# RWKV-7 scan on Trainium2: the triangles of the inversion go through DRAM to one head per partition

## The chip, the cores and the metric

The kernel runs on one core of a Trainium2 chip. The metric is the device time in microseconds of one execution. A run of the kernel is compared with runs of the other kernel on the same chip.

## What is computed

One inference step of a two-layer hybrid trunk over 640 tokens (a prompt of 128 and a sample of 512), width 1024: layer 0 has grouped-query attention beside a Mamba-2 scan, layer 1 a bidirectional RWKV-7 time mixing, and both have a SwiGLU feed-forward part. The change lies in the scan of layer 1, which in the reference is this, for 16 heads of 64, once forward and once backward over the tokens:

```python
def rwkv7_scan(r, w, k, v, kk, a, s0):
    def step(S, inp):
        r_t, w_t, k_t, v_t, kk_t, a_t = inp
        sa = jnp.einsum('bhvk,bhk->bhv', S, kk_t)
        S = (S * w_t[:, :, None, :] - sa[..., None] * (kk_t * a_t)[:, :, None, :]
             + v_t[..., None] * k_t[:, :, None, :])
        return S, jnp.einsum('bhvk,bhk->bhv', S, r_t)
```

## The kernel before

The engines are TensorE (PE; PEld is its weight load), VectorE (DVE), ScalarE (ACT), GpSimd (POOL) and SyncE (SP), which issues most DMAs. Each runs its own stream of instructions in order. The kernel is written in a framework that assigns buffers and sets the order of each engine's stream from the order of the program and from its own costs of instructions; so an edit at one place can move instructions at others.

**The scan in chunks.** The 640 tokens of a direction are cut into five blocks of 128, each of two chunks of 64 (`par` 0 and 1). A chunk is done for all 16 heads at once in matrix form: the recurrence within it becomes a triangular system of 64 equations per head. Work goes by pairs of blocks: block 0 of both directions first (the prompt), then the forward block i with the backward block 5 - i, five pairs in all, numbered 0 to 4.

**`prep` (L1491)** makes what a block needs. It loads the decays into `th` (L1499) and the keys into `kb` (L1508), multiplies `th` by a cumulative matrix (`pc`, L1504), takes exponentials on ACT (L1506 and L1507) into `P` and `Pi`, loads `ar` (L1518) and scales `ar` and `kb` with them (L1520, L1521, L1523; the table `ENGS` says for each whether DVE or POOL does it). Then, per chunk, 32 matmuls give `pS` (L1534), the products of all heads, and DVE multiplies them with a mask (L1536; "the masks", eight per chunk) into the tile `sc`. For three of four pairs of buffers `sc` is a tile of its own, for the others a part of `xt_`, so rows carry either name. Last, `kb` is transposed (`pT`, L1541) and copied to `bt` on ACT (L1542).

**`invert` (L1545)** inverts the 64 triangles of a pair (two directions, two chunks, 16 heads). The two 32x32 diagonal blocks of each go into the buffer `nu`, one head and chunk per partition: 128 partitions are two directions by two halves by 32 heads and chunks. Four DVE stream transposes of 32x1024 (L1555) bring them there from `sc`, where the row index of the triangle lies on the partitions. Then 31 column steps on DVE (a product L1562 and a subtraction L1564 each) build the inverses in `wu`, two more transposes (L1568 into `nu`'s place, L1569) turn them back, and the off-diagonal blocks come from two rounds of small matmuls, `pX` (L1577) and `pW` (L1585), with ACT copies between and after them (L1579, L1589, L1593) that write the inverses back into `sc`. `nu` is read by pX, pW and L1593 until the end of an inversion.

**`chain` (L1595)** is the sequential part: per chunk `pR`, `pU`, `pY`, `pN` on PE with ACT copies between them, and the update of the state `S` on DVE (L1666, L1667). The chain of pair i needs the inverses of pair i and the state of pair i - 1.

**The order.** The driving loop (L1800) interleaves the chain of pair i, the inversion of pair i + 1 and the prep of pairs i + 1 and i + 2 by a string of letters per pair, `SEQS` (L1684); each letter advances one generator by a piece. Pair 0 is prepared and inverted ahead of the loop, while PE computes the values v (`pz`, L1709). In what follows turn i is the stretch in which pair i is inverted, from the end of the column steps of pair i - 1 to the end of its own.

The pool `psc` has two PSUM banks, shared by `pc`, `pT`, `pX` and `pW`.

Of the kernel before, what the change touches and what calls it, by code (L numbers as in the profile page):

```python
# [9 lines left out]
F32 = mybir.dt.float32  # L10
# [78 lines left out]
def _build(ctx, tc, I, O):  # L89
# [38 lines left out]
    thd = dram.tile([2, 5, 128, 1024], F32, name="thd")  # L128
    vd = dram.tile([5, 128, 1024], F32, name="vd")
    yd = dram.tile([2, 10, 64, 1024], F32, name="yd")  # L130
    gd = dram.tile([KT, 128, NT], F32, name="gd")
    xd = dram.tile([128, KT, NT], F32, name="xd")

# [1333 lines left out]
    if True:  # L1467
# [23 lines left out]
        def prep(d, blk, us, bi=0):  # L1491
# [3 lines left out]
            else:  # L1495
                sc = scp[npair[0] // 2 % 2].tile([128, 2, 16, 128], F32, name="sc", tag="sc")
            ap = arp[npair[0] // 2 % 2]
            npair[0] += 1
            load(th, thd[d, blk])  # L1499
            P, Pi, kb = Ps[d], Pis[d], kbs[d]  # L1500
            for q in range(2):
# [8 lines left out]
            for par in range(2):  # L1510
                c = blk * 2 + par
                pl = ap.tile([128, 8, 1], F32, name="pl", tag="pl")
                e = 64 if d == 0 else 1
                G.tensor_copy(pl, P[:, :, par, e:e + 1])
                ar = ap.tile([128, 8, 128], F32, name="ar", tag="ar")
                bk = kb[:, :, par, :]
                o = 0 if d == 0 else 2
                load(ar, rkd[:, :, c].rearrange("p m s t -> p m (s t)"))  # L1518
                ea, eb, ec = ((V, G)[int(z)] for z in ENGS[bi][3 * d:3 * d + 3])
                ea.tensor_tensor(out=ar[:, :, 0:64], in0=P[:, :, par, o:o + 64], in1=ar[:, :, 0:64], op=ALU.mult)  # L1520
                eb.tensor_tensor(out=ar[:, :, 64:128], in0=P[:, :, par, 1:65], in1=ar[:, :, 64:128], op=ALU.mult)  # L1521
                bkv = bk.rearrange("p m (s t) -> p m s t", s=2)
                ec.tensor_tensor(out=bkv, in0=bkv, in1=Pi[:, :, par, :].unsqueeze(2).to_broadcast([128, 8, 2, 64]), op=ALU.mult)  # L1523
                us.append((sc, ar, ap.tile([128, 1024], F32, name="bt", tag="bt"), pl, c, par))
                yield
            for sc, ar, bt, _, _, par in us:
                bk = kb[:, :, par, :]
                for g4 in range(2):

                    pS = [pry.tile([128, 4, 128], F32, name="pS", tag="r") for _ in range(2)]  # L1530
                    for m in range(4):
                        for i in range(2):
                            r = slice(i * 64, i * 64 + 64)
                            T.matmul(pS[i][:, m], bk[r, g4 * 4 + m, :], ar[r, g4 * 4 + m], start=True, stop=True)  # L1534
                    for i in range(2):
                        V.tensor_tensor(out=sc[:, par, g4 * 8 + i:g4 * 8 + 8:2, :], in0=pS[i],  # L1536
                                        in1=msk[d].unsqueeze(1).to_broadcast([128, 4, 128]), op=ALU.mult)
                for g2 in range(2):
                    pT = psc.tile([128, 512], F32, name="pT", tag="s")
                    for m in range(4):  # L1540
                        lastp[0] = T.transpose(pT[:, m * 128:(m + 1) * 128], bk[:, g2 * 4 + m, :], ident)  # L1541
                    S.copy(bt[:, g2 * 512:(g2 + 1) * 512], pT)  # L1542
                yield

        def invert(pairs):  # L1545


            place = ((0, 96), (64, 32))
            G.memset(wu, 0.0)
            G.memset(wu.rearrange("p a b -> p (a b)")[:, 0:1024:33], 1.0)  # L1550
            for g, sc in enumerate(pairs):
                for hf in range(2):
                    r0 = place[g][hf]
                    o = nu[r0:r0 + 32]
                    V.transpose(o if g == 0 else o.rearrange("p j t -> p t j"),  # L1555
                                sc[hf * 32:hf * 32 + 32, :, :, hf * 32:hf * 32 + 32].rearrange("p a h t -> p t (a h)"))
            for j in range(31):
                if j % 8 == 0:
                    yield
# [35 lines left out]
        def chain(us, fresh, ry, keep=False):  # L1595
# [59 lines left out]
            firsts = start_states(pY, hi)  # L1655
            yield
            for d, u in enumerate(us):
                _, _, bt, pl, _, _ = u
                pN = psu.tile([128, 8, 64], F32, name="pN", tag="u")
                for hd in range(16):  # L1660
                    r0 = 64 * (hd % 2)
                    T.matmul(pN[r0:r0 + 64, hd // 2, :], bt[:, hd * 64:(hd + 1) * 64], uvs[d][:, hd, :], start=True, stop=True)
                if fresh:
                    V.tensor_tensor(out=sst[d], in0=pN, in1=pl.to_broadcast([128, 8, 64]), op=ALU.mult)
                else:
                    V.tensor_tensor(out=sst[d], in0=pN, in1=sst[d], op=ALU.add)  # L1666
                    V.tensor_tensor(out=sst[d], in0=sst[d], in1=pl.to_broadcast([128, 8, 64]), op=ALU.mult)  # L1667
                yield
# [25 lines left out]
        uf, ub = [], []  # L1694
        for _ in itertools.chain(prep(0, 0, uf), prep(1, 0, ub)):
            pass
        inv_ = invert((uf[0][0], ub[0][0]))
        for _ in inv_:
            pass

# [99 lines left out]
        for bt_ in range(5):  # L1800
# [30 lines left out]
            for t in SEQS[bt_]:  # L1831
                if t == 's':
                    next(inv_, None)
                elif t == 'i':
                    inv_ = invert((nf[0][0], nb[0][0]))
                    next(inv_)
                elif t == 'j':
                    next(inv_)
# [112 lines left out]
```

## Time and profile before

| | |
|---|---|
| median of three runs | 2121.82 us (2121.23 to 2124.61) |
| profiled execution | 2116.96 us, span of its trace 2115.2 us |
| busy in the span | PE 1950.7 us (92%), DVE 1447.0 (68%), ACT 940.2 (44%), POOL 560.6 (27%) |
| DMA queue of SP and other hardware rings (q1) | 208.87 MB, 32.9% of 16 engines |
| ACT's DMA queue (q10) | 13.11 MB in 17280 packets, 2.0% |

The scan takes some 370 of the 2115 us, from about 1158 to 1530. Shares over the whole span say little of it, because the feed-forward parts and projections on both sides of it are long runs of matmuls. So the rows below are a table of busy time by stage, and the order in time of single engines. In a timeline row the first number is the start, the second the time of the row's instructions together; "[2.43 <-PE pW L1585]" says that the engine sat idle for 2.43 us before it and that PE's pW at line 1585 ended this.

### The profile page before, as it was taken

The page shows a single profiled execution, that of the slowest core. Times are in us where ns is not written, and L with a number is a line of the kernel's source. Part 1 is how long each engine was busy: PE and PEld are TensorE (multiplying, and loading weights), DVE is VectorE, ACT ScalarE, POOL GpSimd, SP SyncE. Part 2 cuts the span into 40 slices and gives each one's busy share as a digit, 9 for nine tenths or more (in the row PEclk, how much of TensorE's full clock was granted, in tenths as well). Part 3 has the DMA queues.
Part 4 walks back from the last instruction along what each step waited for, and adds up shares of the span by engine and source line. Part 5 has one row for each costly group of instructions (what it writes and reads, how often), then busy time and mean ns, then how long its engine had stood idle before and what let it go on. Part 6 is the DMA issues. An engine that isn't in the chain of part 4 may idle for free. (4 is left out here: it accounts for less than half of the span.)

```text
span 2115.2 us, 42931 instructions
## 1 busy us (share of the span) xinstructions
PE 1950.7 (92%) x17701; PEld 1785.1 (84%) x17701; DVE 1447.0 (68%) x2589; ACT 940.2 (44%) x1734; POOL 560.6 (27%) x510
## 2 busy tenths in 40 slices
PE   6999988999999999989999897877789999999998
PEld 5888766989999999969677786867779899999998
DVE  4474666467666758587676839889956787666675
ACT  4333454253433525355555343544463535344351
POOL 2111331002424326031234123313321025243330
PEclk8999999999999999989997988878889899999999
DMA  9764000422433524342466634425344322323221
GB/s 295 220 201 115 7 1 21 149 90 81 130 120 90 162 67 121 108 122 65 148 206 224 202 105 134 123 78 152 100 141 123 120 81 80 100 66 95 61 90 50
DMA packets 256408, 245.72 MB, mean 116 GB/s; under 512 B 27850, under 2 KB 217299, under 8 KB 256085
## 3 DMA queue, kind: packets, MB, share of 16 engines
q1 hardware_dynamic: 233076, 208.87, 32.9%
q0 software_dynamic: 5856, 21.01, 3.0%
q10 hardware_dynamic: 17280, 13.11, 2.0%
q8 instruction: 139, 2.28, 0.5%
q14 instruction: 57, 0.46, 0.1%
HBM read 203.76 MB, written 39.19 MB: 115 GB/s over the span
## 5 line engine op out<-in xcount | busy, mean ns | idle before, releaser
L979 DVE TENSOR_TENSOR ol<-wr,oh 128x512 fp32r<-128x512 f32 x344 | 316.1, 935 | 101.0 <-ACT oh L978 93.6
L978 ACT CAST oh<-wr 128x512 fp32r<-128x512 f32 x344 | 211.3, 619 | 307.1 <-PE d L1130 174.7
L1130 PE MATMUL d<-hid,oh 128*128 128x320 f32 x1312 | 291.3, 310 | 3.6 <-ACT hid L1027 2.5
L1130 PEld LDWEIGHTS d<-hid,oh 128*128 128x128 f32 x1312 | 220.5, 188 | 5.2 <-ACT hid L1027 3.2
L1130 PE MATMUL d<-hid,ol 128*128 128x320 f32 x656 | 203.0, 309 | 0.0
L443 DVE SCALAR_TENSOR_TENSOR x<-d,mod,x 128x128 f32<-128x128 f32 (+2 forms) x204 | 77.2, 433 | 141.6 <-PE d L1130 116.1
L1000 POOL TENSOR_TENSOR g<-wr 128x512 f32<-128x512 f32 x36 | 48.4, 1344 | 460.0 <-DMA wr<-in_ffn_w_up_dram 280.8
L1130 PEld LDWEIGHTS d<-hid,ol 128*128 128x128 f32 x656 | 123.6, 188 | 0.0
L401 PE MATMUL d<-hh,wh 128*128 128x320 f32 (+1 forms) x464 | 118.7, 328 | 3.5 <-ACT hh L435 1.6
L401 PE MATMUL d<-hl,wh 128*128 128x320 f32 (+1 forms) x464 | 114.2, 317 | 3.8 <-POOL hl L436 3.2
L401 PE MATMUL d<-hh,wl 128*128 128x320 f32 (+1 forms) x464 | 112.9, 315 | 0.0
L388 DVE TENSOR_TENSOR wl<-wr,wh 128x1024 fp32r<-128x1024 f32 (+1 forms) x57 | 70.1, 1230 | 56.9 <-ACT wh L386 56.4
L386 ACT CAST wh<-wr 128x1024 fp32r<-128x1024 f32 (+1 forms) x57 | 58.8, 1035 | 105.1 <-PE d L401 65.7
L401 PEld LDWEIGHTS d<-hh,wh 128*128 128x128 f32 (+1 forms) x464 | 79.7, 190 | 17.2 <-ACT at L1385 4.1
L401 PEld LDWEIGHTS d<-hl,wh 128*128 128x128 f32 (+1 forms) x464 | 79.2, 189 | 8.5 <-POOL hl L436 5.9
L1027 ACT CAST hid<-e 128x320 fp32r<-128x320 f32 x88 | 40.5, 460 | 101.4 <-DVE e L1045 100.9
L401 PEld LDWEIGHTS d<-hh,wl 128*128 128x128 f32 (+1 forms) x464 | 79.2, 189 | 1.6 <-DVE wl L388 0.6
L1534 PE MATMUL pS<-ar,ta 64*128 64x128 f32 x640 | 56.4, 311 | 21.4 <-POOL uv L1602 10.2
L1003 POOL TENSOR_TENSOR wr<-wr 128x512 f32<-128x512 f32 x36 | 50.6, 1409 | 84.9 <-DVE ol L979 57.0
L1534 PEld LDWEIGHTS pS<-ar,ta 64*128 64x128 f32 x640 | 48.5, 213 | 28.6 <-POOL uv L1602 11.1
L1005 POOL TENSOR_TENSOR wr<-wr 128x512 f32<-128x512 f32 x36 | 53.3, 1492 | 66.4 <-DVE ol L979 66.4
L1562 DVE TENSOR_TENSOR xt__11664<-ta 128x31 f32<-128x31 f32 (+15 forms) x155 | 66.4, 429 | 4.4 <-ACT ta L1760 0.2
(630 smaller groups left out, 5997.5 us busy)
## 6 DMA issues: line engine op xcount, KB each, us to landing
wt<-in_mod_w_dram SPq DMA_DIRECT2D x80, 512.0 KB, 4.3
wr<-in_ffn_w_gate_dram SPq DMA_DIRECT2D x44, 512.0 KB, 4.4
wr<-in_ffn_w_up_dram SPq DMA_DIRECT2D x44, 512.0 KB, 5.2
wr<-in_ffn_w_down_dram SPq DMA_DIRECT2D x44, 512.0 KB, 4.2
ta<-kbd SPq DMA_DIRECT2D x10, 1024.0 KB, 6.2
ar<-rkd SPq DMA_DIRECT2D x20, 512.0 KB, 5.6
wr<-in_ab_w_in_dram SPq DMA_DIRECT2D x16, 512.0 KB, 7.1
wt<-in_mod_w_dram SPq DMA_DIRECT2D x6, 1024.0 KB, 8.9
```

Of the source, the lines that this page charges most:

```text
L386: S.copy(wh, wr)
L388: V.tensor_sub(wl, wr, wh.bitcast(F32))
L401: T.matmul(ps[b][0:cn, 0:320], w[:, k, 0:cn], a[:, t0:t1], start=(k == 0 and i == 0), stop=(k == w.shape[1] - 1 and i == 2))
L443: V.scalar_tensor_tensor(out=x[:, k, c0:c1], in0=ps[b][:, c0 - 320 * b:c1 - 320 * b], scalar=mod[:, layer, v, gcol + k:gcol + k + 1], in1= ...
L978: S.copy(hi, src)
L979: V.tensor_tensor(out=lo, in0=src, in1=hi.bitcast(F32), op=ALU.subtract)
L1000: E.tensor_tensor(out=g3, in0=a11, in1=a21, op=ALU.add)
L1003: E.tensor_tensor(out=a11, in0=a11, in1=a21, op=ALU.add)
L1005: E.tensor_tensor(out=a12, in0=a12, in1=a11, op=ALU.add)
L1130: T.matmul(bank[:, 0:c1 - c0], p, q, start=i == 0 and z == 0, stop=i == n - 1 and z == 2)
L1534: T.matmul(pS[i][:, m], bk[r, g4 * 4 + m, :], ar[r, g4 * 4 + m], start=True, stop=True)
L1562: V.tensor_tensor(out=tv, in0=nu[:, j + 1:32, j:j + 1].to_broadcast([128, n, j + 1]), in1=wu[:, j:j + 1, 0:j + 1].to_broadcast([128, n, j ...
```

## The change

The tiles of the triangles reach `nu` by way of DRAM instead of by the four DVE transposes. Ten DRAM tiles `nd` are added, one per block and direction, with the layout row, chunk, head, column.

For the backward direction (d = 1), SP writes the masked triangle from `sc` to `nd`, one DMA per chunk in runs of 256 bytes (1024 of them). For the forward direction the triangle is needed transposed, so PE computes the product a second time with its operands exchanged: `pQ`, 16 matmuls of 64x64 per chunk. ACT copies it into `nt`, which is the memory of `th`, and two DMAs of ACT's queue write it to `nd`, in runs of 256 bytes (512 each). No mask is applied to it; the column steps read only the part strictly below the diagonal. `invert` then loads `nu` with four SP DMAs of 32x32x32, in runs of 128 bytes (1024 each). Since `nt` is the memory of `th`, the next load of `th` waits for the two writes out of it; since `nu` is read until the end of the inversion before, its loads wait for that.

In all: 20 DVE transposes fewer; 160 matmuls pQ, 10 ACT copies, 20 DMA issues on ACT and 30 on SP more. Lines behind the edit move by 13 (L1562 becomes L1575, L1666 becomes L1679), those of prep by 3 (L1536 becomes L1539).

```diff
--- before.py
+++ after.py
@@ -128,6 +128,7 @@
     thd = dram.tile([2, 5, 128, 1024], F32, name="thd")
     vd = dram.tile([5, 128, 1024], F32, name="vd")
     yd = dram.tile([2, 10, 64, 1024], F32, name="yd")
+    nd = [dram.tile([64, 2, 16, 64], F32, name=f"nd{i}") for i in range(10)]
     gd = dram.tile([KT, 128, NT], F32, name="gd")
     xd = dram.tile([128, KT, NT], F32, name="xd")
 
@@ -1495,7 +1496,9 @@
             else:
                 sc = scp[npair[0] // 2 % 2].tile([128, 2, 16, 128], F32, name="sc", tag="sc")
             ap = arp[npair[0] // 2 % 2]
+            n_ = nd[npair[0]]
             npair[0] += 1
+            nt = th.rearrange("p (a m s) -> p a m s", a=2, m=8)
             load(th, thd[d, blk])
             P, Pi, kb = Ps[d], Pis[d], kbs[d]
             for q in range(2):
@@ -1521,9 +1524,9 @@
                 eb.tensor_tensor(out=ar[:, :, 64:128], in0=P[:, :, par, 1:65], in1=ar[:, :, 64:128], op=ALU.mult)
                 bkv = bk.rearrange("p m (s t) -> p m s t", s=2)
                 ec.tensor_tensor(out=bkv, in0=bkv, in1=Pi[:, :, par, :].unsqueeze(2).to_broadcast([128, 8, 2, 64]), op=ALU.mult)
-                us.append((sc, ar, ap.tile([128, 1024], F32, name="bt", tag="bt"), pl, c, par))
+                us.append((sc, ar, ap.tile([128, 1024], F32, name="bt", tag="bt"), pl, c, par, n_))
                 yield
-            for sc, ar, bt, _, _, par in us:
+            for sc, ar, bt, _, _, par, _ in us:
                 bk = kb[:, :, par, :]
                 for g4 in range(2):
 
@@ -1535,6 +1538,18 @@
                     for i in range(2):
                         V.tensor_tensor(out=sc[:, par, g4 * 8 + i:g4 * 8 + 8:2, :], in0=pS[i],
                                         in1=msk[d].unsqueeze(1).to_broadcast([128, 4, 128]), op=ALU.mult)
+
+                if d == 0:
+                    pQ = psc.tile([128, 8, 64], F32, name="pQ", tag="s")
+                    for m in range(8):
+                        for i in range(2):
+                            r = slice(i * 64, i * 64 + 64)
+                            T.matmul(pQ[r, m, :], ar[r, m, 0:64], bk[r, m, 0:64], start=True, stop=True)
+                    S.copy(nt[:, par], pQ)
+                    for i in range(2):
+                        nc.scalar.dma_start(out=n_[:, par, i:16:2, :], in_=nt[i * 64:i * 64 + 64, par])
+                else:
+                    load(n_[:, par], sc[0:64, par, :, 0:64])
                 for g2 in range(2):
                     pT = psc.tile([128, 512], F32, name="pT", tag="s")
                     for m in range(4):
@@ -1542,18 +1557,16 @@
                     S.copy(bt[:, g2 * 512:(g2 + 1) * 512], pT)
                 yield
 
-        def invert(pairs):
+        def invert(pairs, nds):
 
 
             place = ((0, 96), (64, 32))
             G.memset(wu, 0.0)
             G.memset(wu.rearrange("p a b -> p (a b)")[:, 0:1024:33], 1.0)
-            for g, sc in enumerate(pairs):
+            for g in range(2):
                 for hf in range(2):
-                    r0 = place[g][hf]
-                    o = nu[r0:r0 + 32]
-                    V.transpose(o if g == 0 else o.rearrange("p j t -> p t j"),
-                                sc[hf * 32:hf * 32 + 32, :, :, hf * 32:hf * 32 + 32].rearrange("p a h t -> p t (a h)"))
+                    r0, b = place[g][hf], slice(hf * 32, hf * 32 + 32)
+                    load(nu[r0:r0 + 32], nds[g][b, :, :, b].rearrange("i a h j -> (a h) i j"))
             for j in range(31):
                 if j % 8 == 0:
                     yield
@@ -1655,7 +1668,7 @@
             firsts = start_states(pY, hi)
             yield
             for d, u in enumerate(us):
-                _, _, bt, pl, _, _ = u
+                _, _, bt, pl, _, _, _ = u
                 pN = psu.tile([128, 8, 64], F32, name="pN", tag="u")
                 for hd in range(16):
                     r0 = 64 * (hd % 2)
@@ -1694,7 +1707,7 @@
         uf, ub = [], []
         for _ in itertools.chain(prep(0, 0, uf), prep(1, 0, ub)):
             pass
-        inv_ = invert((uf[0][0], ub[0][0]))
+        inv_ = invert((uf[0][0], ub[0][0]), (uf[0][6], ub[0][6]))
         for _ in inv_:
             pass
 
@@ -1832,7 +1845,7 @@
                 if t == 's':
                     next(inv_, None)
                 elif t == 'i':
-                    inv_ = invert((nf[0][0], nb[0][0]))
+                    inv_ = invert((nf[0][0], nb[0][0]), (nf[0][6], nb[0][6]))
                     next(inv_)
                 elif t == 'j':
                     next(inv_)
```

The change also moves other instructions. Three places follow, all on DVE.

DVE in turn 1, before: the masks of pair 1 (L1536), the transposes (L1555), and the first column step (L1562, 128x31).

```order
L1536 TENSOR_TENSOR xt__11664<-pS,ta 128x4x128 x8
L1555 STREAM_TRANSPOSE ta<-xt__11664 32x32x32 x2
L1536 TENSOR_TENSOR sc<-pS,ta 128x4x128 x4
L1555 STREAM_TRANSPOSE ta<-sc 32x1024 x2
L1521 TENSOR_TENSOR ar<-ta,ar 128x8x64
L1562 TENSOR_TENSOR xt__11664<-ta 128x31
```

The same place in the changed kernel; L1539 are the masks, L1679 and L1680 the update of the two directions' states in the chain of pair 0, L1575 the column step.

```order
L1539 TENSOR_TENSOR xt__11674<-pS,ta 128x4x128 x8
L1539 TENSOR_TENSOR sc<-pS,ta 128x4x128 x4
L1679 TENSOR_TENSOR S_12769<-pN,S_12769 128x512
L1680 TENSOR_TENSOR S_12769<-S_12769,pl 128x512
L1524 TENSOR_TENSOR ar<-ta,ar 128x8x64 x2
L1679 TENSOR_TENSOR S_12770<-pN,S_12770 128x512
L1680 TENSOR_TENSOR S_12770<-S_12770,pl 128x512
L1539 TENSOR_TENSOR sc<-pS,ta 128x4x128 x3
L1575 TENSOR_TENSOR xt__11674<-ta 128x31
```

The updates, which stood among the later column steps (from the 15th on), now stand ahead of the first, and with them two products of `ar` and three masks of pair 2.

DVE at the start of turn 2, before: the transposes back, the four transposes of the new pair, and the first steps.

```order
L1568 STREAM_TRANSPOSE ta<-ta 128x1024
L1569 STREAM_TRANSPOSE xt__11664<-ta 128x1024
L1555 STREAM_TRANSPOSE ta<-sc 32x32x32
L1555 STREAM_TRANSPOSE ta<-sc 32x1024
L1555 STREAM_TRANSPOSE ta<-sc 32x32x32
L1555 STREAM_TRANSPOSE ta<-sc 32x1024
L1562 TENSOR_TENSOR xt__11664<-ta 128x31
L1564 TENSOR_TENSOR ta<-ta,xt__11664 128x31
L1562 TENSOR_TENSOR xt__11664<-ta 128x60
```

The same place in the changed kernel.

```order
L1581 STREAM_TRANSPOSE ta<-ta 128x1024
L1582 STREAM_TRANSPOSE xt__11674<-ta 128x1024
L1523 TENSOR_TENSOR ar<-ta,ar 128x8x64 x2
L1575 TENSOR_TENSOR xt__11674<-ta 128x31
L1577 TENSOR_TENSOR ta<-ta,xt__11674 128x31
L1679 TENSOR_TENSOR S_12769<-pN,S_12769 128x512
L1575 TENSOR_TENSOR xt__11674<-ta 128x60
L1680 TENSOR_TENSOR S_12769<-S_12769,pl 128x512
L1679 TENSOR_TENSOR S_12770<-pN,S_12770 128x512
L1577 TENSOR_TENSOR ta<-ta,xt__11674 128x30x2
L1680 TENSOR_TENSOR S_12770<-S_12770,pl 128x512
```

The first updates of the chain of pair 1 stood behind the tenth column step and now stand behind the first.

DVE at the start of turn 3 in the changed kernel (before, four masks and four transposes stood here in turn, then the steps, with the updates among the later ones).

```order
L1581 STREAM_TRANSPOSE ta<-ta 128x1024
L1582 STREAM_TRANSPOSE xt__11674<-ta 128x1024
L1539 TENSOR_TENSOR sc<-pS,ta 128x4x128 x3
L1679 TENSOR_TENSOR S_12769<-pN,S_12769 128x512
L1680 TENSOR_TENSOR S_12769<-S_12769,pl 128x512
L1679 TENSOR_TENSOR S_12770<-pN,S_12770 128x512
L1680 TENSOR_TENSOR S_12770<-S_12770,pl 128x512
L1575 TENSOR_TENSOR xt__11674<-ta 128x31
```

Here too the updates come ahead of the first step. Sixteen masks of pair 4, which before stood between L1569 and the first step of turn 4, stand among the steps of turn 3. On ACT, four exponentials of prep that stood ahead of the copies L1593 at the start of turn 2 stand between these copies and ahead of L1579's.

## Rows read from the trace of the kernel before

**Rows 1.** Busy time by stage, turns 1 to 4; the columns are in its first line.
```profile
core 0: us, PE busy (x) PEld busy (x) DVE busy (x) ACT busy (x) POOL busy (x), PEclk, DMA share, GB/s
...
1262.50:1344.80 82.30, 65.80 (x1099) 58.39 (x1097) 76.52 (x122) 27.30 (x49) 30.71 (x31) 0.86 0.52 143
1344.80:1403.30 58.50, 44.72 (x1128) 41.38 (x1129) 51.29 (x88) 29.33 (x42) 20.60 (x22) 0.82 0.38 110
1403.30:1462.10 58.80, 47.98 (x1098) 43.19 (x1096) 48.35 (x86) 32.02 (x47) 13.01 (x11) 0.77 0.29 84
1462.10:1527.30 65.20, 52.55 (x1339) 47.77 (x1334) 59.74 (x120) 30.33 (x45) 25.38 (x24) 0.84 0.42 129
```

**Rows 2.** The view of line 1555: duration min/median/max in ns, first and last start.
```profile
L1555 DVE STREAM_TRANSPOSE ta<-sc x16: 1898/1982/2243, 1179.2 to 1490.4; 32x1024 f32<-32x1024 f32 x16
```

**Rows 3.** Timeline of DVE from the first block to turn 4.
```profile
1264.06 1.76 DVE L1520 TENSOR_TENSOR ar<-ta,ar 128x512 f32<-128x512 f32 x1 [18.96 <-DMA ar<-rkd]
...
1296.84 0.20 DVE L1562 TENSOR_TENSOR xt__11664<-ta 128x31 f32<-128x31 f32 x1
...
1317.10 0.68 DVE L1666 TENSOR_TENSOR S<-pN,S 128x512 f32<-128x512 f32 x1
...
1344.81 1.25 DVE L1568 STREAM_TRANSPOSE ta<-ta 128x1024 f32<-128x1024 f32 x1
...
1356.76 1.96 DVE L1555 STREAM_TRANSPOSE ta<-sc 32x1024 f32<-32x1024 f32 x1 [2.43 <-PE pW L1585]
1358.85 0.20 DVE L1562 TENSOR_TENSOR xt__11664<-ta 128x31 f32<-128x31 f32 x1
...
1366.75 0.69 DVE L1666 TENSOR_TENSOR S<-pN,S 128x512 f32<-128x512 f32 x1 [0.66 <-PE pN L1662]
...
1427.58 0.21 DVE L1562 TENSOR_TENSOR xt__11664<-ta 128x31 f32<-128x31 f32 x1
...
1473.85 4.88 DVE L1536 TENSOR_TENSOR sc<-pS,ta 128x512 f32<-128x512 f32 x8 [0.42 <-PE pS L1534]
...
1492.60 0.20 DVE L1562 TENSOR_TENSOR xt__11664<-ta 128x31 f32<-128x31 f32 x1 [0.24 <-ACT ta L1760]
```

**Rows 4.** Timeline of PE in turn 1.
```profile
1265.63 2.49 PE L1650 MATMUL pU<-uv,sc 64*64 64x64 f32 x64
...
1303.98 2.09 PE L1662 MATMUL pN<-uv,bt 128*64 128x64 f32 x64
...
1318.86 1.91 PE L1859 MATMUL p<-ca,S 128*64 128x128 f32 x8 [10.93 <-DVE S L1667]
```

**Rows 5.** Timeline of ACT at the start of turn 2.
```profile
1345.70 0.60 ACT L1506 ACTIVATE ta<-pc 128x512 f32<-128x512 f32 x1
1346.18 0.70 ACT L1507 ACTIVATE ta<-pc,lnh 128x512 f32<-128x512 f32 x1
1346.75 4.08 ACT L1593 COPY sc<-ta 32x1024 f32<-32x1024 f32 x2
...
1356.56 0.59 ACT L1589 ACTIVATE sc<-pW 32x512 f32<-32x512 f32 x1
```

**Rows 6.** Instructions by line, 1158.5 to 1560: count | busy us, mean ns | idle before.
```profile
L1562 DVE TENSOR_TENSOR xt__11664<-ta 128x31 f32<-128x31 f32 (+15 forms) x155 | 66.4, 429 | 4.4 <-ACT ta L1760 0.2
L1564 DVE TENSOR_TENSOR ta<-ta,xt__11664 128x31 f32<-128x31 f32 (+15 forms) x155 | 63.9, 412 | 4.2
...
L1536 DVE TENSOR_TENSOR sc<-pS,ta 128x512 f32<-128x512 f32 x64 | 40.8, 679 | 6.0 <-PE pS L1534 6.0
...
L1542 ACT COPY bt<-pT 128x512 f32<-128x512 f32 x40 | 21.9, 588 | 92.7 <-PE pT L1541 92.0 <-PE pN L1662 0.7
```

**Rows 7.** DMA issues: queue, count, KB each, median us from issue to landing.
```profile
ar<-rkd SPq DMA_DIRECT2D x20, 512.0 KB, 5.6
...
rkd<-kt ACTq DMA_DIRECT2D x8, 320.0 KB, 3.3
...
vd<-vv ACTq DMA_DIRECT2D x20, 128.0 KB, 2.1
...
wr<-in_rwkv_w_dram SPq DMA_DIRECT2D x4, 256.0 KB, 4.0
```

**Rows 8.** DMA queues on the page: packets, MB, share of 16 engines' time.
```profile
q1 hardware_dynamic: 233076, 208.87, 32.9%
```

## The prediction, made before the changed kernel ran

> **What bounds the kernel now.** I read the stages of the scan first. The change touches nothing before the triangles of pair 0 and nothing after the last inversion, so the table by stage says where it can matter. A "turn" below is the stretch from the end of one inversion's column steps to the end of the next: turn 1 inverts pair 1 while the chain of pair 0 runs, and so on to turn 4. The reader is to see that no engine fills a turn: VectorE (DVE) is busy 76.52 of 82.3 us in turn 1 (93%), 51.29 of 58.5 and 48.35 of 58.8 in turns 2 and 3, 59.74 of 65.2 in turn 4, and TensorE has 66 of 82 in turn 1 and 45 to 53 of 59 to 65 after it [rows 1]. DVE is nearest to the limit, and a turn ends with its last column step, so a turn is "gap until the first column step" plus "run of 31 steps with other work between them".
>
> Second, the view of the removed line: 16 of the 20 transposes are of this form, median 1982 ns [rows 2] (the other four move the same shape), so four of an inversion hold DVE 8.0 us, 32 us over turns 1 to 4, and 8 more ahead of the turns. Third, DVE's order of time [rows 3]: the first column step stands at 1296.84, 1358.85, 1427.58 and 1492.60, and the state update of the chain (L1666) comes after it, at 1317.10 in turn 1, at 1366.75 in turn 2. Fourth, TensorE in turn 1 [rows 4]: pN, on which that update waits, runs from 1303.98 for 2.09 us, yet TensorE goes on at 1318.86, 10.93 us idle on DVE's update. So in turn 1 DVE did column steps while the chain waited for it. In turn 2 it is the other way: DVE reaches the update and waits 0.66 us for pN [rows 3]. There the chain's path (last step, pX, pW, copies, pR, pU, pN, update) and DVE's own work end almost together.
>
> **The change part by part.**
>
> *Removed:* 8.0 us of DVE per inversion. Where the transposes stand alone on the path this is all gain; in turns 2 and 4 only the last one does, 1.96 us after a wait of 2.43 us for pW in turn 2 [rows 3], since the buffer nu is read by pX and pW of the inversion before.
>
> *Added on TensorE and ACT:* 16 small matmuls of pQ per chunk, 160 in all. The nearest row has 64 of the same 64x64 form in 2.49 us [rows 4], so 0.6 us per chunk, 1.2 per pair. One ACT copy of 128x512 from PSUM per chunk at 588 ns [rows 6]. TensorE's idle time in every turn and ACT's (it is busy 27 to 32 us of a turn [rows 1]) hide both: 0; uncovered, they would cost 1.8 us per pair, at most 7 over the four turns.
>
> *Added on the queues:* a round trip through DRAM. The write has runs of 256 bytes; the nearest row, the kt writes with 256-byte runs, takes 3.3 us for 320 KB. The load has runs of 128 bytes, a form that the trace does not show; the nearest in packets is the load of 256 KB in 1024 packets, 4.0 us, with 2.1 (a 128 KB write) and 5.6 (a 512 KB load) as ends [rows 7]. I take 4.0, by the count of packets. So 7.3 us stand against the 8.0 of the transposes when nothing covers the trip, and the last load's 4.0 against one transpose of 2.0 where only that was exposed. By themselves these come to nearly nothing; what decides is the order that now surrounds the wait.
>
> The Trainium skill, page "DMA: Bandwidth & Descriptors", section Specifications, speaks against the change: it wants transfers of at least 512 B and says that below this the engine reads, modifies and writes. The trace does not bear out a large loss: 256-byte runs moved 320 KB in 3.3 us where 512-byte runs moved 512 KB in 5.6 [rows 7], much the same rate. If the rule doubled my 4.0, the sum below would be 4 us more, since in turn 4 the load would end that much later, while in turn 2 the state update covers it.
>
> *First block.* DVE waits 18.96 us for a load of ar there, and starts at 1264.06 [rows 3]; the inversion of pair 0 lies long before that, so a later start of it is covered: 0, ends -1 and +2.
>
> *Turn 1.* The four state updates, two ar products and three masks now stand ahead of the first column step, which waited for none of them before. pN ends at 1306.1 [rows 4], perhaps 4 us sooner, as two transposes no longer stand ahead of the masks that pR waits for; I take 1304. Nine operations of some 0.65 us (a mask takes 679 ns [rows 6]; next to others they follow at a little less) put the first step at 1310 against 1296.84. Steps cost (66.4 + 63.9) / 5 = 26.1 us per inversion [rows 6]; the order puts twenty other such operations between them, 13 us: end 1349, against 1344.81. Undisturbed steps, without the slow ones that a busy GpSimd beside them makes, would save some 3.5, pN sooner or later 2. **+3** (ends -1 and +5). The 10.93 us that TensorE gets back here is in that figure: it brings the update forward, but not the steps.
>
> *Turn 2.* One step stands ahead of the updates where there were ten. DVE idles through the chain's path, to 1366.75 before; and four exponentials of 0.6 to 0.7 us, which ACT had done before the inverse's copies [rows 5], now stand between those copies and ahead of the copies of pX: +2.5, so 1369.3, and 1371.9 after four updates. The rest of the run is 25.7 of steps, four more updates (2.6), two products of kb (2.4) and 13 masks (8.5, of which five came later before): 39, end 1411 against 1403.3. Undisturbed steps take 3.5 off. **+6** (ends +4 and +8). The nu load is covered here: nu is free after pW, near 1361, plus 4.0 is before 1369.
>
> *Turn 3.* The updates again stand ahead of the first step, so the gap is that of turn 2, some 27 us in place of 24.3 (1403.3 to 1427.58): +2.8. Sixteen masks of pair 4, which had stood in the gap of turn 4 (eight take 4.88 us [rows 3]), move into this run: 16 x 0.65 = +10.4, less up to 2.6 for updates that left the run. **+12** (ends +10 and +13).
>
> *Turn 4.* The masks are out of its gap, and so are three of four transposes' worth that ran under pX and pW. Before, the first step was 30.5 us after the turn's start; now the path to pW (14 us in turn 2, by the start of L1589 at 1356.56 and four copies of 0.6 [rows 5]), the nu load with its issue (4.4) and TensorE's other work, some 3 to 5 us, end it: 22. That is -8.5, and about -1 in the run. **-9.5** (ends -12 and -5).
>
> **Sum:** 0 + 3 + 6 + 12 - 9.5 = **+11.5**, between +1 and +21. The profiled execution took 2116.96 us, so 2128.5; the median of the runs shown, 2121.82, is 4.9 above it, so **2133**.
>
> **The rivals.**
>
> *Faster: DVE was the bound and is relieved.* The place is turn 1 (93% busy) and turns 2 and 4. If updates that come early let the next matmuls, masks and chains start early, the idle time is not lost but moved; TensorE's 10.93 us of idle speak for it. At most 32 us; the 2.43 us wait and the load that replaces a transpose take back some 2 to 4 per turn, so about -20: 2102. It decides if turn 2's gap stays under 20 us. Against it: DVE does idle in the new order, behind a chain that is no shorter.
>
> *No change.* The round trip costs what the transposes cost (7.3 against 8.0), and the masks that move from turn 4 to turn 3 cancel: 0 +- 4, 2122. The spread of turns 2 and 3 above speaks against it.
>
> *Much slower: the small transfers crowd the queues.* There are 10 writes of 1024 pieces, 20 of 512 and 20 loads of 1024, 41,000 packets beside 233,076 [rows 8], almost all within 350 us, on engines that are busy 0.29 to 0.52 there [rows 1]. If the four loads of a turn go one behind the other (16 us in place of 4) and the load of th, which now waits for the transfers out of its own buffer, comes late too, turns 1, 3 and 4 lose some 8 each more: +35, 2157.
>
> The Trainium skill, page "VectorE: DVE Perf Modes", in its Rules for kernel authors, calls the DVE transpose the fastest for 32x32 within a bank. Here that is 2.0 against 7.3 for one trip, and by it the change loses 5.3 wherever the trip is exposed; exposed in turns 1 and 3 that is +11 more, inside this last rival.
>
> That the change does not do what it says I leave out: the order of instructions shows the transposes gone and the loads in their place.
>
> **How the numbers follow.** My sum, 0.52 (its own range 2123 to 2143); faster rival 0.20; no change 0.10; crowding 0.18. About 4.2 us, 0.2%, is what a measurement of this kernel can tell from no change. Of my sum's case 0.42 lies above that, 0.06 within and 0.04 below; of the no-change case some 0.02 lies above and 0.01 below. Slower 0.62, same 0.13, faster 0.25. The range that leaves out about 2 in 10 reaches from 2106, into the faster rival, to 2156, almost to the slowest.
>
> **What would show it.** In the changed kernel's DVE timeline: no transposes before the first step; the first step of turn 1 near 1310, updates of L1666's successor just ahead of or behind the first step; turn 2 of 64 to 65 us, turn 3 near 71, turn 4 near 56. nd writes should land in 2 to 6 us and nu loads in about 4. DVE should be about 40 us less busy. Wrong: turn 2 with a gap under 20 us, nu loads over 8 us, or a first column step that waits for DMA in turns 1 or 3.

## The result, and the profile after

The changed kernel takes 2154.81 us in the median of four runs (2150.52 to 2168.68), the kernel before 2122.9 beside it: a ratio of 1.0159, interval 1.0123 to 1.0194, some 33 us slower. The side was the one forecast; the size, 11.5 us, was a third of it, so that the time lies 1 us inside the upper end of the range (2106 to 2156), an end that came from the crowding rival, and beyond the sum's own (2123 to 2143). The two profiled executions differ by a little more, 2153.9 against 2115.2 us of span.

Busy time by turn, the cuts at the ends of the column steps as in [rows 1]; the columns are those of rows 1.

```profile
1267.00:1357.95 90.95, 63.71 (x1206) 57.03 (x1205) 63.52 (x119) 24.69 (x44) 28.16 (x26) 0.86 0.66 163
1357.95:1424.34 66.39, 51.90 (x1111) 47.94 (x1110) 44.49 (x90) 31.76 (x45) 20.25 (x22) 0.75 0.35 86
1424.34:1504.30 79.96, 62.03 (x1430) 56.80 (x1430) 57.18 (x103) 34.89 (x51) 25.08 (x22) 0.83 0.54 144
1504.30:1569.29 64.99, 41.52 (x1058) 38.53 (x1058) 43.96 (x91) 29.00 (x41) 15.75 (x14) 0.67 0.31 91
```

DVE is less busy in every turn but the third, and every turn but the fourth is longer. Turn by turn, against 82.3, 58.5, 58.8 and 65.2: turn 1 ends 13.1 us later than before (1357.95 for 1344.81), of which 3.1 stem from the first block; turn 2 is 7.9 longer, turn 3 21.2, turn 4 0.2 shorter. The part behind the scan gives 3.3 back. The inversion of pair 0, ahead of the turns, ends 19.4 us later (1244.80 for 1225.45); the first state update of that pair does not (1275.68 for 1276.31), so this delay is covered. TensorE's granted clock is lower in turns 2 and 4 (0.75 and 0.67, before 0.82 and 0.84), but its busy time per matmul over the four turns is the same (45.6 ns against 45.3), so nothing here speaks for a slower TensorE as the cause.

DVE's timeline shows where it sat. The steps are L1575, the updates L1679, the masks L1539; [rows 3] has the first steps before.

```profile
1267.11 0.69 DVE L1523 TENSOR_TENSOR ar<-ta,ar 128x512 f32<-128x512 f32 x1 [19.25 <-DMA ar<-rkd]
...
1298.89 0.69 DVE L1679 TENSOR_TENSOR S<-pN,S 128x512 f32<-128x512 f32 x1 [11.85 <-PE pN L1675]
...
1303.22 1.29 DVE L1524 TENSOR_TENSOR ar<-ta,ar 128x512 f32<-128x512 f32 x2 [2.91 <-ACT ta L1509]
...
1311.78 1.29 DVE L1539 TENSOR_TENSOR sc<-pS,ta 128x512 f32<-128x512 f32 x2 [5.57 <-PE pS L1537]
...
1314.09 0.20 DVE L1575 TENSOR_TENSOR xt__11674<-ta 128x31 f32<-128x31 f32 x1
...
1376.34 0.21 DVE L1575 TENSOR_TENSOR xt__11674<-ta 128x31 f32<-128x31 f32 x1 [6.95 <-DMA ta<-nd]
1384.35 0.69 DVE L1679 TENSOR_TENSOR S<-pN,S 128x512 f32<-128x512 f32 x1 [7.46 <-PE pN L1675]
...
1448.86 0.69 DVE L1679 TENSOR_TENSOR S<-pN,S 128x512 f32<-128x512 f32 x1 [19.73 <-PE pN L1675]
...
1451.52 0.20 DVE L1575 TENSOR_TENSOR xt__11674<-ta 128x31 f32<-128x31 f32 x1
...
1528.55 0.69 DVE L1679 TENSOR_TENSOR S<-pN,S 128x512 f32<-128x512 f32 x1 [5.44 <-PE pN L1675]
1529.16 0.20 DVE L1575 TENSOR_TENSOR xt__11674<-ta 128x31 f32<-128x31 f32 x1
```

Whoever looks for the new DMAs in the waits finds them once: 6.95 us in turn 2. In every turn DVE sits in front of an update, waiting for pN, with all of the 31 steps behind it, in turn 2 all but one. That reads as if the order alone were the loss. The runs say otherwise.

Prices of the added work, from the DMA issues (queue, count, KB each, median us to landing) and the instructions by line:

```profile
ta<-kbd SPq DMA_DIRECT2D x10, 1024.0 KB, 7.1
ar<-rkd SPq DMA_DIRECT2D x20, 512.0 KB, 7.1
...
vd<-vv ACTq DMA_DIRECT2D x20, 128.0 KB, 3.4
nd<-ta ACTq DMA_DIRECT2D x20, 128.0 KB, 3.7
ta<-nd SPq DMA_DIRECT2D x20, 128.0 KB, 3.9
...
nd<-sc SPq DMA_DIRECT2D x6, 256.0 KB, 4.8
nd<-xt__11674 SPq DMA_DIRECT2D x4, 256.0 KB, 3.6
```

The load of `kb` before:

```profile
ta<-kbd SPq DMA_DIRECT2D x10, 1024.0 KB, 6.2
```

The added instructions and the column steps of the changed kernel:

```profile
L1577 DVE TENSOR_TENSOR ta<-ta,xt__11674 128x31 f32<-128x31 f32 (+15 forms) x155 | 73.8, 476 | 3.9
L1575 DVE TENSOR_TENSOR xt__11674<-ta 128x31 f32<-128x31 f32 (+15 forms) x155 | 62.2, 402 | 10.7 <-DMA ta<-nd 7.0
...
L1547 PE MATMUL pQ<-ta,ar 64*64 64x64 f32 x320 | 12.3, 230 | 1.1 <-ACT sc L1602 1.1
...
L1548 ACT COPY ta<-pQ 128x512 f32<-128x512 f32 x10 | 5.9, 587 | 28.3 <-PE pQ L1547 22.6 <-DMA vd<-vv 5.7
```

### The profile page after: what moved, and what is told of

Its sections match the earlier page's. It is cut to its first block, busy times and chain, and to the rows that moved or that the text cites. A ratio compares the mean times of both kernels' runs of the same rounds, so it can differ in the third digit from the quotient of the medians.

```text
span 2153.9 us, 43650 instructions
## 1 busy us (share of the span) xinstructions
PE 1963.1 (91%) x18021; PEld 1800.1 (84%) x18021; DVE 1404.0 (65%) x2569; ACT 947.7 (44%) x1744; POOL 563.4 (26%) x510
## 5 line engine op out<-in xcount | busy, mean ns | idle before, releaser
L980 DVE TENSOR_TENSOR ol<-wr,oh 128x512 fp32r<-128x512 f32 x344 | 305.5, 904 | 102.2 <-ACT oh L979 94.2
L387 ACT CAST wh<-wr 128x1024 fp32r<-128x1024 f32 (+1 forms) x57 | 58.8, 1035 | 112.8 <-PE d L402 61.4
L1577 DVE TENSOR_TENSOR ta<-ta,xt__11674 128x31 f32<-128x31 f32 (+15 forms) x155 | 73.8, 476 | 3.9
L1537 PEld LDWEIGHTS pS<-ar,ta 64*128 64x128 f32 x640 | 48.6, 212 | 32.1 <-DVE sc L1539 10.5
```

The lines of the kernel that those rows point to most:

```text
L387: S.copy(wh, wr)
L980: V.tensor_tensor(out=lo, in0=src, in1=hi.bitcast(F32), op=ALU.subtract)
L1577: V.tensor_tensor(out=wu[:, j + 1:32, 0:j + 1], in0=wu[:, j + 1:32, 0:j + 1], in1=tv, op=ALU.subtract)
```

## The experiments

Ratios are to the kernel before, run on the same chip. Figures in us beside a ratio are worked out from it. Three theories were set against each other: the order (updates ahead of the first step), the DMAs (latency and crowding), and the buffer (the load of th waits for the writes out of its memory).

**The order undone in the changed kernel.** The product of each column step is kept in a list, and the update is tied to one of them:

```diff
-                    V.tensor_tensor(out=sst[d], in0=pN, in1=sst[d], op=ALU.add)
+                    k_ = behind[0] if c_ == cw else None
+                    with contextlib.nullcontext() if k_ is None else tc.issue_after(cst_[k_].ins):
+                        V.tensor_tensor(out=sst[d], in0=pN, in1=sst[d], op=ALU.add)
...
-... bababAsiCCjABAjCCjjB ...
+... bababAsijjCCABAjCCjB ...
```

> The changed kernel with its data path untouched, but the state updates of the chain's first chunk (in turn 1 of its second) queued on DVE behind column step 15, 11, 15 and 12 of the running inversion, as they stood before, by an order edge and by tracing the steps of turn 2 ahead of the chain. Order theory (the loss comes from updates that stand ahead of the first column step, so that DVE idles through the chain's path): most of the 32 us comes back, 2105 to 2132 us. DMA theory (the loss is the latency and the crowding of the small transfers): the steps then wait for the loads instead and the time stays at 2145 or more. Buffer theory (the loss comes from the load of th, which waits for the writes out of its own memory): also 2145 or more.

2149.89 us, 1.0135 (1.0114 to 1.0157): five of 33 us come back, not told apart from nothing, as the intervals overlap. In the trace the updates do stand where they stood before (the first behind step 15, 11, 15 and 12), so the order theory alone falls. DVE in turns 1, 2 and 4 of this run:

```profile
1307.13 1.29 DVE L1526 TENSOR_TENSOR ar<-ta,ar 128x512 f32<-128x512 f32 x2 [15.36 <-ACT ta L1511]
1314.90 1.29 DVE L1541 TENSOR_TENSOR sc<-pS,ta 128x512 f32<-128x512 f32 x2 [6.48 <-PE pS L1539]
...
1377.41 0.21 DVE L1578 TENSOR_TENSOR xt__11674<-ta 128x31 f32<-128x31 f32 x1 [10.49 <-DMA ta<-nd]
...
1522.57 0.20 DVE L1578 TENSOR_TENSOR xt__11674<-ta 128x31 f32<-128x31 f32 x1 [10.98 <-DMA ta<-nd]
```

The waits for pN are gone, and waits for the loads of nu (10.49, 10.98) and for an exponential of the next pair (15.36) stand in their place.

**The order alone, on the kernel before.** The first step is tied behind the last update, and the chain's letters are traced first:

```diff
+                with contextlib.nullcontext() if j or lasts[0] is None else tc.issue_after(lasts[0].ins):
...
-aaaCbabCbbbaAsACijjABjBCj bababAsiCCjABAjCCjjB babbsaijACBjBjACCACj abbbasijojCCjoCojooC
+aaaCbabCbbbaAsACiCjjABjBj bababAsiCCjABAjCCjjB babbsaiACBCjjBjACACj abbbasiCCjojjoCojooC
```

> The kernel before, with its transposes, but the state updates placed ahead of the first column step in turns 1 to 4, as the changed kernel has them, by an order edge and by tracing the chain's pieces ahead of the steps. Order theory: slower by 20 to 40 us, 2143 to 2163. DMA theory and buffer theory: no DMA is added, so within 6 us of 2122.9.

2143.98 us, 1.0104 (1.0086 to 1.0121), some 22 us. The order is a real cost with the transposes in place, and the expectation holds at its lower edge. So it costs much alone, and taking it away from the changed kernel gives little: something else takes its place there.

**The buffer.** `nt = ta[:, 2112:3136]` (the forward Pi) in place of `th`.

> The changed kernel, but ACT copies pQ into the memory of the forward Pi, which is dead by then, in place of th's: the next load of th no longer waits for the two writes. Buffer theory: 10 to 20 us come back, 2135 to 2145. Order theory and DMA theory: 0 to 6 us come back, 2149 to 2156; the updates still stand ahead of the first step or just behind it.

2151.77 us, 1.0147 (1.0118 to 1.0176): 2 to 3 us, not told apart from nothing.

**The added work, with the transposes kept.** First all of it but the loads:

```diff
+                if d == 0:
+                    pQ = psc.tile([128, 8, 64], F32, name="pQ", tag="s")
...
+                    S.copy(nt[:, par], pQ)
...
+                else:
+                    load(n_[:, par], sc[0:64, par, :, 0:64])
```

> The kernel before, with its transposes, plus the added work alone: pQ, its ACT copies into th's memory, and all writes to the DRAM tiles; nothing is loaded from there. The order of steps and updates stays close to that before. Order theory: within 6 us of 2122.9. DMA theory: the loads are half of the loss, so 5 to 15 us slower. Buffer theory: 10 to 20 us slower, since the load of th waits here as well.

2138.09 us, 1.008 (1.0056 to 1.0104), 17 us slower, though nothing reads what is written. That is beyond the order theory's 6 and fits the buffer theory best. It is not the order again: in this trace the updates stand behind the same steps as before, give or take two. Then its parts: pQ and the copies without any DMA; SyncE's writes without pQ; all writes, with the copy in Pi.

> The kernel before plus pQ and its copies into th's memory alone; no DMA is added, nothing reads the copy. The added work with all its writes cost 15 us. If the matmuls and copies (TensorE, ACT and the two PSUM banks that they share with pc, pT, pX, pW) are the cause: 8 to 15 us slower than 2122.6. If the writes are (queue theory or buffer theory): within 5 us of it.

> The kernel before plus SyncE's ten writes of the backward triangles alone, without pQ; nothing is loaded. Queue theory (loads of prep stand behind writes that wait for the masks on SyncE's queue): 8 to 15 us slower than 2122.6. Otherwise within 5 us of it.

> The kernel before plus all the added work but the loads, as in the fourth run, with the copy of pQ in the dead memory of the forward Pi in place of th's. Buffer theory: the 15 us mostly go, 2122 to 2130. Queue theory and the theory of matmuls and copies: 2133 to 2140, as the fourth run.

2127.18 us, 1.003 (1.0016 to 1.0044), 6 us; 2124.91, 1.0026 (1.001 to 1.0043), 5 us; 2132.99, 1.0056 (1.0036 to 1.0076), 12 us. The first two stay within 5 us of 2122.6, the smaller of their expectations; the last falls between its two, at the foot of the higher. Three small costs would add up: about 6 (3 to 9) for matmuls and copies, 5 (2 to 9) for SyncE's writes, and the remaining 5 or 6 for ACT's writes and the wait of th's load. How that remainder divides is not shown: Pi takes 5 away, but the intervals of the runs with and without it overlap. One place where the matmuls and copies of pQ cost time is the start of turn 2 of the run with pQ alone (DVE, PE, then ACT; L1579 is the last transpose back, L1587 pX, L1603 the inverse's copies). A chunk's pQ is 32 records of TensorE, 1.15 us there.

```profile
1346.82 1.92 DVE L1579 STREAM_TRANSPOSE xt__11674<-ta 128x1024 f32<-128x1024 f32 x1
```

```profile
1353.30 3.33 PE L1507 MATMUL pc<-ta 128*128 128x128 f32 x16 [3.00 <-ACT bt L1552]
...
1357.35 0.22 PE L1587 MATMUL pX<-xt__11674,sc 32*32 32x32 f32 x1
```

```profile
1350.91 1.92 ACT L1603 COPY xt__11674<-xt__11674 32x1024 f32<-32x1024 f32 x1
1352.63 1.09 ACT L1552 COPY bt<-pT 128x512 f32<-128x512 f32 x2
```

Before:

```profile
1345.97 2.14 DVE L1569 STREAM_TRANSPOSE xt__11664<-ta 128x1024 f32<-128x1024 f32 x1
```

```profile
1348.26 0.21 PE L1577 MATMUL pX<-xt__11664,sc 32*32 32x32 f32 x1 [1.85 <-DVE xt__11664 L1569]
```

With pQ in the program, pT and pc run between the last transpose and pX; pc waits for a PSUM bank until ACT, behind the inverse's copies of 2 us, has copied pT out. pX starts 10.5 us after the last transpose begins, against 2.3 before. At this place it is displacement, not work. The changed kernel shows little of it: in its turn 2 pX starts 6.5 us into the turn (before 3.5), and in turns 3 and 4 it starts 3.2 us into the turn, as soon as the transposes back end, where before it started at 7.6 and 20.1 us. TensorE in these last two turns:

```profile
1427.51 0.21 PE L1590 MATMUL pX<-xt__11674,sc 32*32 32x32 f32 x1 [3.89 <-DVE xt__11674 L1582]
...
1507.48 0.23 PE L1590 MATMUL pX<-xt__11674,sc 32*32 32x32 f32 x1 [6.19 <-DVE xt__11674 L1582]
```

So where the added work costs its time in the changed kernel stays open.

**Both together, with transposes.** The last two edits in one.

> The kernel before plus all the added work but the loads, with the updates ahead of the first column step as in the second run. Two causes that add: 15 + 21, so 2155 to 2163, and then transposes against loads in that order is worth nothing or a gain of a few us (the changed kernel has 2154.8). Causes that overlap (the early updates leave slack in which the added work hides): 2140 to 2150, and the loads cost some 5 to 15 on top.

2166.61 us, 1.0217 (1.0181 to 1.0252), 46 us, above even the range for causes that add (2155 to 2163): 22 and 17 are 39. Beside the run with the order alone, the added work costs 24 us in the changed kernel's order. With updates leading, loads in place of transposes then look like a gain of 12 us (1.0217 to 1.0159, though the intervals touch); with steps leading they are a loss of 12 (1.008 to 1.0135, intervals apart).

**Half of the change.** Backward triangles through DRAM, forward ones by their two transposes, no pQ:

```diff
-                    load(nu[r0:r0 + 32], nds[g][b, :, :, b].rearrange("i a h j -> (a h) i j"))
+                    if g:
+                        load(nu[r0:r0 + 32], nds[g][b, :, :, b].rearrange("i a h j -> (a h) i j"))
+                    else:
+                        V.transpose(nu[r0:r0 + 32], pairs[0][b, :, :, b].rearrange("p a h t -> p t (a h)"))
```

> Half of the change: the backward triangles go through DRAM (SyncE's write, two loads per inversion), the forward ones keep their two transposes; no pQ, no ACT copy, no write out of th's memory. The order falls as the framework sets it; here the updates stay behind the tenth step in turns 2 to 4, and lead only in turn 1. If what costs is pQ with its copies and the buffer of th: 2118 to 2130, since two transposes cover the two loads. If any load from DRAM on the path of an inversion costs more than the transposes: 2133 to 2145.

> The half as before, with the order edges of the first run, so that the updates stand behind the steps in turn 1 as well. If the order of the updates is worth something beside the half: 3 to 10 us faster than the half. If the two transposes already cover the loads in every turn: within 4 us of it, and no slower than 2128.

2120.23 us, 0.9993 (0.998 to 1.0007): no difference from before, inside the lower expectation. With the order edges of the first run 2112.0, **0.9949 (0.993 to 0.9967)**, 11 us faster than before and 8 faster than without them, as expected if the order is worth something: the best version of the study. DVE in its turn 1:

```profile
1286.88 3.99 DVE L1565 STREAM_TRANSPOSE ta<-sc 32x1024 f32<-32x1024 f32 x2
1290.90 2.19 DVE L1526 TENSOR_TENSOR ar<-ta,ar 128x512 f32<-128x512 f32 x2
1296.69 0.35 DVE L1572 TENSOR_TENSOR xt__11674<-ta 128x31 f32<-128x31 f32 x1 [3.60 <-DMA ta<-nd]
```

The two transposes run while the two loads are under way; 3.60 us of waiting remain here and 4.48 in the inversion of pair 0, while in turns 2 to 4 the first step waits for no load. The kernel before has its updates behind these steps already, and with edges of this kind, though not just these, it does not gain (below); so it is hardly the edges alone.

**All repairs of the changed kernel, and the same order before.** Updates behind the steps, the copy in Pi, and in turn 1 the products and masks of pair 2 tied behind the third step (`tc.issue_after(cst_[2].ins)`); then the same edges and letters with the transposes, without the change.

> The changed kernel with three repairs together: the updates behind the steps (first run), pQ's copy in the dead Pi (third run), and in turn 1 the products of ar and the masks of pair 2 behind the third column step. In the first run DVE waited 15.4 us for an exponential ahead of such products in turn 1, and 6.5 for their masks. If these three waits are the loss beside the added work: 2122 to 2137. If the data path itself loses (loads and added work on the path in every turn): 2140 or more.

> The kernel before, with its transposes, and the same edges and letters as the last run: what the order alone is worth there. Expected within 5 us of 2122.6, as the order before already had the updates behind the steps; if the last run gains much by a better order, this one should gain as well (2110 to 2118).

2155.36 us, 1.0155 (1.0136 to 1.0174), and 2124.77, 1.0009 (0.9995 to 1.0022). The first run misses its lower range by 18 us and falls under "the data path itself loses": the repairs gain nothing. The second is as expected. DVE, ACT's queue and SyncE's queue in turn 1 of the first:

```profile
1290.56 2.49 DVE L1547 TENSOR_TENSOR sc<-pS,ta 128x512 f32<-128x512 f32 x4 [0.52 <-PE pS L1544]
1307.46 1.41 DVE L1584 TENSOR_TENSOR xt__11674<-ta 128x31 f32<-128x31 f32 x1 [14.41 <-DMA ta<-nd]
```

```profile
1292.55 0.59 ACT L1556 COPY ta<-pQ 128x512 f32<-128x512 f32 x1 [2.44 <-PE pQ L1555]
1293.12 0.59 ACT L1565 COPY bt<-pT 128x512 f32<-128x512 f32 x1
1293.18 1.27 ACTq L1558 DMA_DIRECT2D nd<-ta  x2
```

```profile
1297.23 5.71 SPq L104 DMA_DIRECT2D ta<-nd  x4
```

This is the bare trip, with nothing in front of the step but the loads: from the copy of pQ at 1292.55 to the step at 1307.46 it takes 14.9 us. The copy takes 0.59, two issues on ACT 1.27 us, four on SyncE with their waits 5.71, and the landing of write and load the rest.

**The other half.** Forward triangles through DRAM, backward by transposes, with the edges of the faster half, and without them; and the changed kernel with the writes of pQ's copy issued by SyncE.

> The other half of the change: the forward triangles go through DRAM (pQ, its ACT copy into th's memory, ACT's writes, two loads), the backward ones keep their two transposes, with the order edges of the tenth run. If the forward route itself is the loss (its matmuls, copies, ACT's issues and the wait of th's load): 2128 to 2145, far above the tenth run's 2112. If the loss is that nothing covers the loads once all four transposes are gone: 2112 to 2122, as here too two transposes stand beside two loads.

> The same half without the order edges; the framework then puts the updates ahead of the first step in turns 1 and 3, behind the sixth in turn 2 and the fourth in turn 4. If the order costs here what it cost with transposes: 8 to 20 us above the run before it.

> The changed kernel with the writes of pQ's copy issued by SyncE in place of ACT. If ACT's time for the issues (20 of some 0.6 us, between the copies of an inversion) is a large part of the loss: 5 to 12 us faster than 2154.8. If it is not: within 5 us, or slower, as loads then stand behind these writes on SyncE's queue.

2145.0 us, 1.0106 (1.0091 to 1.0121); 2153.73, 1.0149 (1.0118 to 1.018); 2154.88, 1.0148 (1.0117 to 1.0178). The two halves with the same edges are 33 us apart (2112 against 2145), although both have two loads and two transposes per inversion. The first is at the upper edge of what was expected if the forward route is the loss, the second 8.7 us above it, also as expected, though the two intervals touch. So the forward route carries the loss; in the full change it does not matter who issues its writes (2154.88 against 2154.81). DVE's waits from 1262 to 1560 in the forward half (us in total, times, longest), then the same two in the backward half, then SyncE's queue in turn 1 of the forward half:

```profile
DVE ar L1526 <- ACT ta L1511: 14.6, 2, 9.7
DVE xt__11674 L1579 <- DMA ta<-nd: 13.4, 2, 10.0
```

```profile
DVE xt__11674 L1572 <- DMA ta<-nd: 3.6, 1, 3.6
...
DVE ar L1526 <- ACT ta L1511: 0.8, 1, 0.8
```

```profile
1301.43 0.34 SPq L104 DMA_DIRECT2D ta<-thd  x1
1301.82 2.11 SPq L104 DMA_DIRECT2D ta<-nd  x2
```

These two waits make 28.0 us in one half and 4.4 in the other. The forward triangle starts later (behind its pS, on the same engine), goes over ACT, and holds th's memory until its writes land. The wait for an exponential of the next pair would follow from the late load of th; that was not tried in the half, and in the full change another memory for the copy gave back 2 to 3 us, not told apart from nothing.

## Why the prediction came out as it did

**The step that failed** is that TensorE's idle time in every turn and ACT's "hide both: 0", and with it the writes, which had no term of their own. The added work costs 17 us in the order before and 24 in the order of the changed kernel. Most single prices were right: the copy 587 ns against 588, the load 3.9 us against 4.0, the writes 3.6 to 4.8 and 3.7 against 3.3. The matmuls of a chunk took 1.15 us against 0.6 (the trace has 320 records where I counted 160). The bound for uncovered work, 1.8 us per pair and 7 in all, was too low: it has that half price and one copy of the pair's two. With the busy time of the trace (12.3 and 5.9 us in ten chunks) it is 3.6 per pair and 14.6 over the four turns. pQ and its copies alone cost 6, so part of them was hidden, but not all; the rest of the 17 came with the writes. The cover was not there: idle time in a turn is not idle time at the place where the work falls. Where that place lies in the changed kernel is not shown.

**The order term was about right in its sum.** Order and removed transposes, +11.5, have their measured counterpart in 22 for the order alone, less the some 12 that loads instead of transposes give in that order: 10, with an uncertainty about as large, since the intervals behind the 12 touch. That DVE would idle through the chain's path in the new order is what the waits for pN show (11.85, 7.46, 19.73 and 5.44 us).

**By turns**, +3, +6, +12 and -9.5 were forecast, and 10.0, 7.9, 21.2 and -0.2 came, with +3.1 for the first block, where I had 0. In turn 1 the first step came at 1314.09, 4 us behind the 1310 worked out, 3.1 of them from the first block; this was partly luck, as the first update came 5 us earlier than the 1304 taken for pN, and waits of 2.91 and 5.57 us, which were not foreseen, came after it. The run was 43.9 us, not 39. Turn 2 is as worked out without the discount for undisturbed steps (1411 against 1403.3), and so is the gap of turn 3 (1424.34 to 1451.52 is 27.2; forecast 27). Turn 3's run was 52.8 us (1451.52 to 1504.30) against 34.6 before; the timeline has 30 other operations among the steps where it had 9, not 16 more, and eight slow steps where it had three. Turn 4's gap was 24.9, not 22, because an update stands ahead of its first step too, which I had left out there; its run was 40.1 against 34.7 before, with three slow steps. The ends of the terms add up to 0 and 23, not 1 and 21 as the prediction has it; neither reaches 33. Of the signs named, DVE is 43 us less busy (forecast 40), the loads of nu land in 3.9 us, and no first step waits for DMA in turns 1 and 3. The gap of turn 2 to its first step is 18.4 us, under the 20 that were to speak for "faster"; but the steps behind it stand after an update that comes 26.4 us into the turn, so the sign was badly chosen.

**The round trip**, 7.3 us in the prediction, is 14.9 in the run where nothing else stands before the step. The sum of two landings leaves out four issues in a row on one queue and what each of them waits for.

**The rivals.** "Faster" falls: DVE was relieved (1447.0 to 1404.0 us busy) and the scan grew. "No change" falls. "Crowding" has nearly the right time (2157) by luck: the place was wrong and only part of the mechanism right. Loads beside the new transfers land later (kb 7.1 against 6.2 us, ar 7.1 against 5.6 [rows 7]), and SyncE's writes cost 5 us. The load of th in turn 1 does come late, but sparing it that wait gave nothing clear. The loads of nu land in 3.9 us, and what costs in the halves is the forward route, not the count of packets. The Trainium skill ("DMA: Bandwidth & Descriptors", Specifications) gives 512 B as the least transfer for full rate. The traces show little of that at equal size: in the changed kernel 128 KB in 256-byte runs land in 3.7 us, and `vd<-vv`, 128 KB in 1024-byte runs, in 3.4; the 2.1 of `vd<-vv` before [rows 7] was without the new transfers beside it. That the DVE transpose is fastest for 32x32 (the Trainium skill, "VectorE: DVE Perf Modes", Rules for kernel authors) holds against the bare trip, 8 against 14.9 us, and did not decide: in the best version half of the blocks go through DRAM, with two transposes beside two loads.

One change at a time leads from the kernel before to the changed one: the order costs 22 us, the added work in that order 24, and loads in place of transposes give some 12 back, which makes some 33. The first two are clear of noise, the third only just. Not tried apart was which of the forward route's parts (its place behind pS, the banks, the loads at its end) makes how much of the loss; another memory for the copy and another engine for the issues, tried singly, changed nothing clear.

## What to carry to other kernels

Here a trip through DRAM in place of work on a busy engine paid only for the half that needed no added matmuls, with as much work left on the engine to cover it; it is worth trying half. Do not put added work at nothing because its engines have idle time somewhere in the stretch; run it once with the old path kept, which shows its price at once. And when a wait vanishes on undoing an order, look at what the time did before calling the order the cause.

## What the runs showed that I had not expected

A DMA issue with 512 runs took ACT's queue 647 ns in the median (582 to 1470, 20 issues of `nd<-ta`), about as long as a copy of 128x512 (587). Two costs that were each within a few microseconds of nothing (1.003 and 1.0026) are part of a sum of 17, and order edges of a kind that gains nothing before (1.0009) go with a gain of 8 us in the half.
